# A hybrid decoder block: w_in multiplied with whole float32 numbers, the parameter chain early on VectorE, another order of the mixers' steps, narrow outputs

## Chip, cores and metric

One core of a Trainium2 chip runs one launch of the kernel. The metric is the device time of that launch in microseconds (us): for the kernel before, the median of three runs, 1183.16 us (1183.14 to 1184.67).

## What is computed

One trunk layer over 256 positions, model width 2048, in float32:

```
proj = rmsnorm(x, g1) @ w_in                     # 2048 x 3072: rg_u, rg_gate, s5_u, 1024 each
u  = causal_conv4(rg_u)                          # RG-LRU group, 16 heads of 64
r, i = sigmoid(u @ wa + ba), sigmoid(u @ wi + bi)
a  = exp(-8 r softplus(-lam));  h = scan(a, sqrt(1 - a^2) * i * u)
y_rg = gelu(rg_gate) * h
Abar = exp(A dt);  h = scan(Abar, ((Abar - 1) / A) B s5_u)   # S5 group, 64 groups of 64 complex states
y  = real(C h) + d * s5_u;  z = gelu(y);  y_s5 = z * sigmoid(z @ w_glu + b_glu)
x += concat(rmsnorm(y_rg), rmsnorm(y_s5)) @ w_out            # 2048 x 2048
h  = causal_conv3(rmsnorm(x, g2) @ w_up)                     # 2048 x 12288
x += (gelu(h[:6144]) * h[6144:]) @ w_down                    # 6144 x 2048
out = rmsnorm(x, gf)
```

## The kernel before

Channels lie on the 128 partitions, the 256 positions along the row. A weight matrix is cut into column tiles of 128 outputs; SyncE's queue loads it in blocks `raw` of 8 row tiles (128x1024 numbers, 512 KB) into four buffers. Exactness is kept by halves: ScalarE rounds a block to float32r (`wh`, L151), VectorE takes the remainder (`wl`, L154), and the activations are split the same way into a pair of high and low (`split`, L192 to L199). One row tile of a product, a *step*, is then either wide, one matmul of `wh` with both halves (128x512, L159) and one of `wl` with the high half (128x256, L163), or narrow, three matmuls of 128x256 (L161 to L163). The wide form leaves two halves in PSUM, which `total` adds (ScalarE copy L169, VectorE add L170). The letters in WIDE choose the form by matrix: A w_in, W and V the two halves of w_out, L w_glu, F w_up, D w_down. Steps: w_in 384, w_glu 64, w_out 256, w_up 1536, w_down 768.

The mixers' work is written as letters in ORDER, a letter with a tile's number: U a column of rg_u with its convolution, P its gates (`pg`), B decay and input of the recurrence for four tiles, G recurrence and gate column, S a column of s5_u, X the sines, T the tile's cosine and sine tables (six GpSimd operations), K its matrices (16 GpSimd operations `m`, `ball`, `cp`, transposes `tp`, products `cb`, and eight small loads `u4`), N the input `bu` and the scan, Y the output `y`, F and Z gelu and split, L the w_glu column, W and E, V the two halves of an output column; R and Q the two norms. The order is one of priority: a scheduler with its own idea of times places each instruction in its engine's in-order queue, so what `order` rows show below is fixed when the program is built. Before the tiles comes a chain of small operations on the parameters (L360 to L470), which gives the decay, the angles and the factors `fr`, `fi`, `nfr` that T and K read; its first exponential (`exp_parts`, called with G) runs on GpSimd. The first four columns of w_in (HEAD) take turns while x arrives in quarters `xq`; their PSUM tiles are all four buffers of `main`. x's squares are summed to `acc1`, and `rstd1` comes out of a product on TensorE (`ss`), a square root and a reciprocal.

Of the kernel before, what the change touches and what calls it, by code (L numbers as in the profile page):

```python
# [14 lines left out]
P = 128  # L15
# [14 lines left out]
# The mixers' steps in the order of their priority: a letter of block_kernel's steps and a tile's number.  # L30
ORDER = """
U0 P0 S0 U1 P1 U2 S1 X0 U3 T0 T1 P2 P3 U4 U5 S2 B0 U6 P4 U7 S3 P5 S4 K0 P6 P7 T2 B1 K1 N0 N1 Y0 S5 T3 Y1 F0 G0
K2 G1 G2 S6 T4 G3 G4 K3 F1 N2 T5 Y2 N3 G5 G6 Y3 F2 G7 S7 F3 K4 N4 R0 K5 N5 W0 Y4 T6 W1 W2 Y5 K6 Z0 Z1 E0 E1 W3
E2 E3 Z2 K7 Z3 F4 W4 E4 F5 W5 E5 N6 W6 E6 W7 E7 T7 W8 E8 N7 Y6 W9 Y7 W10 W11 E9 Z4 F6 E10 E11 Z5 W12 F7 E12 Z6
Z7 L0 W13 E13 L1 W14 E14 L2 L3 W15 L4 E15 L5 L6 L7 Q0 V0 V1 V2 V3 V4 V5 V6 V7 V8 V9 V10 V11 V12 V13 V14 V15
"""
# The columns of w_in that the first loads feed, and the order of those loads: a quarter of x or a block of w_in.
# [11 lines left out]
def _top(v, bits):  # L49
# [10 lines left out]
    ("g1", KX), ("g2", KX), ("gf", KX),  # L60
# [3 lines left out]
    ("logdt", NST), ("lam", KH), ("are", NST), ("aim", NST),  # L64
    ("step", NX + NY), ("ident", P),
]
COL = {}
# [8 lines left out]
def block_kernel(ctx, tc, a, out):  # L76
# [9 lines left out]
    # ---------------------------------------------------------------- constants  # L86
    par = cpool.tile([P, NCOL], F32, name="par")
    S.dma_start(par[:, :KX], a["par"][:, :KX])
# [13 lines left out]
    WIDE = "FDAWVL"  # L102
# [4 lines left out]
    CUT, CUT_END = 4, 3  # L107
# [8 lines left out]
    def fn(out, src, func, **kw):  # L116
        """An activation that needs its own table: these stay in program order, so that equal ones are neighbours."""
        ins = S.activation(out, src, func, **kw).ins  # L118
        if last_fn:
            tc.add_manual_dep(ins, last_fn[0].name, mybir.DependencyInfo(  # L120
                mybir.DependencyClass.NoSync, mybir.DependencyReason.DATA), reason="table order")
        last_fn[:] = [ins]

    # ------------------------------------------------------------- weight stream
    due = []

    def later(n, fn):
        """fn is emitted behind n more products."""
        due.append([n, fn])
# [18 lines left out]
    pieces = [1]  # L148

    def part(raw, wh, wl, k=slice(0, KC)):  # L150
        S.copy(wh[:, k, :], raw[:, k, :])  # L151
        n = (k.stop - k.start) // pieces[0]
        for i in range(k.start, k.stop, n):
            V.tensor_tensor(wl[:, i:i + n, :], raw[:, i:i + n, :], wh[:, i:i + n, :].bitcast(F32), ALU.subtract)  # L154

    def step(ps, wide, wh, wl, kk, x, first, last):
        """Adds w.T x of 128 rows; wide puts w_high x_low beside the rest."""
        if wide:
            PE.matmul(ps, lhsT=wh[:, kk, :], rhs=x, start=first, stop=False)  # L159
        else:  # L160
            PE.matmul(ps[:, 0, :], lhsT=wh[:, kk, :], rhs=x[:, 0, :], start=first, stop=False)  # L161
            PE.matmul(ps[:, 0, :], lhsT=wh[:, kk, :], rhs=x[:, 1, :], start=False, stop=False)  # L162
        PE.matmul(ps[:, 0, :], lhsT=wl[:, kk, :], rhs=x[:, 0, :], start=False, stop=last)  # L163
# [9 lines left out]
    def product(src, ot, kcs, xs, wide=False):  # L173
        """w.T x; a caller that wants it in PSUM takes the narrow one."""
# [3 lines left out]
        for kc in kcs:  # L178
            raw = load(src, ot, kc)
            wh, wl = w_parts()  # L180
            part(raw, wh, wl)
            for kk in range(KC):
                step(ps, wide, wh, wl, kk, xs[j], j == 0, j == n - 1)
                j += 1
        flush()
# [16 lines left out]
    def rstd(parts_, dim, tag):  # L202
        """1 / rms over the channels for every position, on all partitions; without a tag it stays in PSUM."""
# [17 lines left out]
    def rstd_direct(acc, dim, tag):  # L221
        """The same with one step on the tensor engine, more on the vector engine."""
# [17 lines left out]
    # ------------------------------------------------------------- split x  # L240
    # products that nobody reads raise the tensor engine's clock while the first loads run
# [5 lines left out]
    for name in HEAD_LOADS.split():  # L247
        if name == "p":
            nc.sync.dma_start(par[:, KX:], a["par"][:, KX:])
            continue  # L250
# [5 lines left out]
        else:  # L256
            if o == 0:
                raw0[i] = wpool.tile([P, KC, P], F32, tag="raw", name="raw", bufs=4)
            nc.sync.dma_start(raw0[i][:, o:o + n, :], a["w_in"][HEAD[i % len(HEAD)], i // len(HEAD), :, o:o + n, :])

    def x_split(k):
        xs.append(split(cpool, f"x{k}", xq[k // 4][:, k % 4, :], col("g1", k), V if k in XV else S))

    # ===================================================================== mixers
    with ExitStack() as ph:
# [3 lines left out]
        # the first columns' products take turns by the rows of x, as these arrive  # L269
        early = {c: psm.tile([P, 2, T], F32, tag="main", name="ps") for c in HEAD}  # L270
        acc1 = mix.tile([P, 4, T], F32, tag="e4", name="acc1")
        for i in range(2 * len(HEAD)):
            kc, ci = divmod(i, len(HEAD))
            ps = early[HEAD[ci]]
            wh, wl = w_parts()
            n = KC // 2 if ci == 0 else KC
            for r in range(0, KC, n):
                ks = range(KC * kc + r, KC * kc + r + n)
                if ci == 0:
                    x_split(ks[0])  # L280
                part(raw0[i], wh, wl, slice(r, r + n))
                if ci == 0:
                    for k in ks[1:]:
                        x_split(k)
# [5 lines left out]
                for k in ks:  # L290
                    step(ps, "A" in WIDE, wh, wl, k % KC, xs[k], k == 0, k == KX - 1)
# [4 lines left out]
        # short steps let the chain of small ones on the parameters through  # L296
        pieces[0] = CUT

        # -------------------------------------------------- small parameter math
        ahead = tc.high_priority(offset=PRI)  # L300
        ahead.__enter__()
        # what the scans' tiles hold before them
# [12 lines left out]
        def stt(e, out, x, c, y, op0, op1):  # L315
            """(x op0 c) op1 y"""
# [46 lines left out]
        p0, s0, s1 = exp_parts(G, e_in, nE, "d")  # L363
        ex = tl(nE, "ex")
        stt(G, ex, p0, 1.0, s0, ALU.add, ALU.mult)
        G.tensor_tensor(ex, ex, s1, ALU.mult)
# [6 lines left out]
        # angle of one step, into [-pi, pi]  # L373
# [9 lines left out]
        # angle of a block of steps, in turns, as a short part and its rest; the four state tiles of a channel tile as s5_scan has them  # L383
# [9 lines left out]
        # cosine and sine at the multiples of NY blocks and at those below it  # L393
# [29 lines left out]
        # decay of a block, in s5_scan's order of the state tiles  # L423
# [7 lines left out]
        # powers 3, 2, 1 of A  # L431
# [13 lines left out]
        def times(ore, oim, xre_, xim_, yre, yim, t):  # L445
            """A product of complex numbers; t has the place of two."""
# [9 lines left out]
        # factors of b by the position in the block: A^(3 - position) (A - 1) / a; the real part negated as well  # L456
# [29 lines left out]
        def s5_tables(c):  # L486
            """Cosine and sine at every block."""
# [12 lines left out]
        def s5_mats(c):  # L500
# [7 lines left out]
            # b for the four positions, [imaginary, tile, channel, position]  # L508
# [9 lines left out]
            # c A^3, c A^2, c A  # L518
# [27 lines left out]
            # a head's channels by position in the rows, two heads at a time  # L546
# [54 lines left out]
        # softplus(-lambda) times -4  # L601
# [16 lines left out]
        # ------------------------------------------------------------- the mixers' steps  # L618
# [10 lines left out]
        def w_in_col(o):  # L629
            wide = "A" in WIDE  # L630
            return total(early[o] if o in early else product(a["w_in"], o, (0, 1), xs, wide), wide)

        def rg_u(j):
            """Column tile j of u, and its convolution."""
            if j == CUT_END:
                pieces[0] = 1
# [12 lines left out]
        def rg_gates(j):  # L649
            """Its two gates; r in tau, i times u in bu."""  # L650
# [12 lines left out]
        def rg_batch(g):  # L663
            """Decay and input of the recurrence, for four tiles."""
# [6 lines left out]
            # 1 / (1 - tanh) is (1 + a) / 2: one Newton step from the exponential's (1 + a) / 2; it and h come out negated  # L671
# [9 lines left out]
        def rg_out(j):  # L681
            """The recurrence, the gate's column tile and their product."""
# [25 lines left out]
        def rg_top(o):  # L708
            """The RG-LRU half of the output's column tile o."""
# [24 lines left out]
        def s5_top(o):  # L734
            """The S5 half, and the second norm's input."""
# [22 lines left out]
    # ======================================================================== FFN  # L758
# [48 lines left out]
# ---- layout of the arrays for the launch  # L807
# [87 lines left out]
```

## Time and profile before

| | |
|---|---|
| median of the timed runs | 1183.16 us |
| profiled execution, span from first to last instruction | 1181.2 us |
| TensorE busy | 1119.9 us (95%) |
| VectorE, ScalarE, GpSimd busy | 892.4, 641.0, 270.8 us |
| mean granted TensorE clock | 0.98 |
| chain that ended last | TensorE 80%, GpSimd 9%, VectorE 7% |

The page gives busy time by engine, and the chain of work that ended last, followed back from the last instruction. TensorE's matmuls overlap in the records, so their busy times add up to more than the span; how long a step takes is read from the distance of starts. Everything outside the first third (slices 1 to 11 of 40) shows TensorE at nine tenths and more.

### The profile page before, as it was taken

What the parts mean: (1) busy time and instruction counts of PE and PEld (TensorE: products, weight loads), DVE (VectorE), ACT (ScalarE), POOL (GpSimd) and SP (SyncE); (2) the same over time, 40 slices, a digit from 0 to 9 for tenths busy, and PEclk for the clock granted to TensorE, in tenths of its full rate; (3) what the DMA queues carried; (4) which work ended last, traced back from release to release, by engine and by line L of the source; (5) the groups of instructions that cost most, each with busy time, mean ns of one, the idle gap of its engine ahead of it and who ended that gap; (6) DMA issues with size and microseconds to landing.
All of it is one profiled execution on the core that took longest, in us unless ns stands there. A gap on an engine that the chain in (4) does not pass through costs nothing.

```text
span 1181.2 us, 18986 instructions
## 1 busy us (share of the span) xinstructions
PE 1119.9 (95%) x7134; PEld 973.9 (82%) x7134; DVE 892.4 (76%) x1356; ACT 641.0 (54%) x1014; POOL 270.8 (23%) x300
## 2 busy tenths in 40 slices
PE   7887869879999999999999999999999999999996
PEld 6775658767888888888888888888888888888886
DVE  6899999997899887787787777877876444445443
ACT  6475655534876655555555555555554444344432
POOL 6368997893333000000000000000000000000000
PEclk8999889999999999999999999999999999999998
DMA  7554336443656666666666666666666666666662
GB/s 255 163 168 136 109 118 195 143 131 99 196 178 191 187 193 189 189 193 186 191 193 187 190 194 186 192 192 187 192 191 185 189 184 187 187 186 190 183 191 90
DMA packets 65980, 209.25 MB, mean 177 GB/s; under 512 B 12000, under 2 KB 15584, under 8 KB 65888
## 3 DMA queue, kind: packets, MB, share of 16 engines
q1 hardware_dynamic: 65744, 208.03, 58.5%
q8 instruction: 56, 0.92, 0.3%
q14 instruction: 36, 0.29, 0.1%
q10 hardware_dynamic: 144, 0.01, 0.0%
HBM read 204.87 MB, written 2.10 MB: 175 GB/s over the span
## 4 chain that ended last, share of the span: by engine, by line
PE 80%; POOL 9%; DVE 7%; issue 2%; ACT 1%; DMA 1%; SPq 0%; DVEq 0%; POOLq 0%; ACTq 0%
PE ps L159 51%; PE ps L163 27%; DVE wl L154 2%; POOL cp L528 1%; DVE wa L574 1%; POOL m L516 1%; POOL ball L517 1%; DVE xq L685 1%; ACT wh L151 1%; DMA xq<-in_xT 1%; POOL m L515 1%; POOL m L525 0%; PE ps L162 0%; DVE rcv L643 0%; PE ps L161 0%
## 5 line engine op out<-in xcount | busy, mean ns | idle before, releaser
L159 PE MATMUL ps<-sp,wh 128*128 128x512 f32 x2960 | 1043.9, 396 | 3.8 <-ACT wh L151 1.9
L163 PE MATMUL ps<-sp,wl 128*128 128x256 f32 x3008 | 851.3, 283 | 18.2 <-DVE wl L154 18.2
L159 PEld LDWEIGHTS ps<-sp,wh 128*128 128x128 f32 x2960 | 558.4, 189 | 130.0 <-DVE sp L199 2.5
L154 DVE TENSOR_TENSOR wl<-raw,wh 128x1024 fp32r<-128x1024 f32 (+2 forms) x384 | 478.5, 1248 | 234.4 <-ACT wh L151 232.7
L151 ACT CAST wh<-raw 128x1024 fp32r<-128x1024 f32 (+1 forms) x378 | 395.0, 1046 | 411.2 <-PE ps L159 286.2
L163 PEld LDWEIGHTS ps<-sp,wl 128*128 128x128 f32 x3008 | 572.3, 190 | 25.9 <-DVE wl L154 23.7
L236 POOL TENSOR_TENSOR accx<-accx,sq 128x256 f32<-128x256 f32 x29 | 37.7, 1301 | 793.6 <-ACT sq L235 793.5
L770 DVE SCALAR_TENSOR_TENSOR cv<-u,par,cv 128x255 f32<-128x255 f32 x192 | 92.1, 481 | 3.7 <-ACT cv L768 0.3
L170 DVE TENSOR_TENSOR t<-t,ps 128x256 f32<-128x256 f32 x160 | 65.7, 412 | 0.1
L169 ACT COPY t<-ps 128x256 f32<-128x256 f32 x160 | 57.8, 363 | 10.0 <-DVE u L720 7.6
L768 ACT ACTIVATE cv<-u,par 128x256 f32<-128x256 f32 x96 | 57.1, 596 | 1.4 <-DVE u L766 1.4
L766 DVE TENSOR_TENSOR u<-t,rstd 128x256 f32<-128x256 f32 x96 | 40.4, 421 | 1.6
L528 POOL TENSOR_TENSOR cp<-m,m 64x192 f32<-64x192 f32 x32 | 31.1, 973 | 1.9
L788 DVE TENSOR_TENSOR xq<-xq,ps 128x256 f32<-128x256 f32 x31 | 13.0, 421 | 16.4 <-PE ps L163 15.9
L721 POOL TENSOR_TENSOR xq<-xq,u 128x256 f32<-128x256 f32 x16 | 18.0, 1127 | 26.4 <-DVE u L720 20.8
L118 ACT ACT_TABLE_LOAD x17 | 21.8, 1283 | 1.4 <-PEq L884 1.2
L780 DVE TENSOR_TENSOR hv<-ge,cv 128x256 f32<-128x256 f32 x48 | 20.4, 426 | 1.9 <-issue 0.2
L118 ACT ACTIVATE ge<-cv 128x256 f32<-128x256 f32 x48 | 20.1, 419 | 0.2
L193 DVE TENSOR_TENSOR sp<-hv,sp 128x256 fp32r<-128x256 f32 x48 | 20.1, 419 | 0.0
L531 ACT COPY bp<-ball 64x128 f32<-64x128 f32 x16 | 6.8, 423 | 24.3 <-POOL ball L517 24.2
L192 ACT CAST sp<-hv 128x256 fp32r<-128x256 f32 x48 | 19.5, 406 | 0.0
L199 DVE SCALAR_TENSOR_TENSOR sp<-xq,par,sp 128x256 fp32r<-128x256 f32 x32 | 15.6, 521 | 1.5 <-ACT sp L198 1.5
(245 smaller groups left out, 654.2 us busy)
## 6 DMA issues: line engine op xcount, KB each, us to landing
raw<-in_w_up SPq DMA_DIRECT2D x192, 512.0 KB, 4.3
raw<-in_w_down SPq DMA_DIRECT2D x96, 512.0 KB, 4.3
raw<-in_w_in SPq DMA_DIRECT2D x47, 512.0 KB, 4.2
raw<-in_w_out SPq DMA_DIRECT2D x32, 512.0 KB, 4.1
raw<-in_w_glu SPq DMA_DIRECT2D x8, 512.0 KB, 4.1
xq<-in_xT SPq DMA_DIRECT2D x7, 512.0 KB, 6.0
out_y<-xq SPq DMA_DIRECT2D x6, 256.0 KB, 2.1
rw<-in_rgw SPq DMA_DIRECT2D x8, 128.0 KB, 3.5
```

The source lines that it names most:

```text
L118: ins = S.activation(out, src, func, **kw).ins
L151: S.copy(wh[:, k, :], raw[:, k, :])
L154: V.tensor_tensor(wl[:, i:i + n, :], raw[:, i:i + n, :], wh[:, i:i + n, :].bitcast(F32), ALU.subtract)
L159: PE.matmul(ps, lhsT=wh[:, kk, :], rhs=x, start=first, stop=False)
L163: PE.matmul(ps[:, 0, :], lhsT=wl[:, kk, :], rhs=x[:, 0, :], start=False, stop=last)
L169: S.copy(t, ps[:, 1, :])
L170: V.tensor_tensor(t, t, ps[:, 0, :], ALU.add)
L236: G.tensor_tensor(acc, acc, q, ALU.add)
L528: G.tensor_tensor(cp[rp, :BL - 1, m, :, 16 * h:16 * h + 16], m1[rp], m2[rp], op)
L766: V.tensor_tensor(u, ps, rs["n2"], ALU.mult)
L768: S.activation(cv, u, AF.Identity, bias=col("fcb", o), scale=col("fcw", 2 * 2 * KF + o))
L770: V.scalar_tensor_tensor(cv[:, d:], u[:, :T - d], col("fcw", (2 - d) * 2 * KF + o), cv[:, d:], ALU.mult, ALU.add)
```

## The change

All 384 steps of w_in take the loaded block as it is: one float32 matmul of 128x256, without `wh`, `wl` and without splitting x (`x_scale` only multiplies by g1). w_glu and w_out become narrow (WIDE is "FD"), so their results are read from PSUM without `total`. The columns that the parameter chain reads move to the front of `par`, in the first load on ScalarE's queue (136 columns instead of 16; the second load, on SyncE's queue, has 632 instead of 752). The first exponential runs on VectorE. The cutting of `wl` into pieces (CUT) goes. ORDER is another.

```diff
-U0 P0 S0 U1 P1 U2 S1 X0 U3 T0 T1 P2 P3 U4 U5 S2 B0 U6 P4 U7 S3 P5 S4 K0 P6 P7 T2 B1 K1 N0 N1 Y0 S5 T3 Y1 F0 G0
+U0 X0 S0 P0 U1 P1 T0 K0 U2 P2 S1 N0 Y0 U3 P3 B0 T1 K1 U4 P4 S2 N1 Y1 U5 P5 T2 K2 U6 P6 S3 N2 Y2 U7 P7 B1 T3 K3 F0
...
-    ("g1", KX), ("g2", KX), ("gf", KX),
+    ("g1", KX), ("logdt", NST), ("lam", KH), ("are", NST), ("aim", NST), ("step", NX + NY),
+    ("g2", KX), ("gf", KX),
...
-    S.dma_start(par[:, :KX], a["par"][:, :KX])
+    S.dma_start(par[:, :NFIRST], a["par"][:, :NFIRST])
...
-    WIDE = "FDAWVL"
+    WIDE = "FD"
...
+    def product_whole(src, ot, kcs, x):
+        ps = psm.tile([P, T], F32, tag="main", name="ps")
+        n = len(kcs) * KC
+        for i, kc in enumerate(kcs):
+            raw = load(src, ot, kc)
+            for kk in range(KC):
+                j = KC * i + kk
+                PE.matmul(ps, lhsT=raw[:, kk, :], rhs=x[j], start=j == 0, stop=j == n - 1)
+        flush()
+        return ps
...
+    def x_scale(k):
...
+        if k in XV:
+            V.tensor_scalar(xs[k], src, col("g1", k), None, ALU.mult)
+        else:
+            S.activation(xs[k], src, AF.Copy, scale=col("g1", k))
...
-                    step(ps, "A" in WIDE, wh, wl, k % KC, xs[k], k == 0, k == KX - 1)
+                    PE.matmul(ps, lhsT=raw0[i][:, k % KC, :], rhs=xs[k], start=k == 0, stop=k == KX - 1)
...
-        p0, s0, s1 = exp_parts(G, e_in, nE, "d")
+        p0, s0, s1 = exp_parts(V, e_in, nE, "d")
...
-            wide = "A" in WIDE
-            return total(early[o] if o in early else product(a["w_in"], o, (0, 1), xs, wide), wide)
+            return early[o] if o in early else product_whole(a["w_in"], o, (0, 1), xs)
```

TensorE's queue, before, where tile 0's `cb` and `bu` stand (`u` the tile's input, rows with `sp` and `wh` or `wl` are halves of steps):

```order
L159 MATMUL ps<-sp,wh 128x512
L163 MATMUL ps<-sp,wl 128x256
L541 MATMUL cb<-cp_511,bp_510 32x96 x8
L562 MATMUL bu<-u_1217,bt 64x64 x16
L163 MATMUL ps<-sp,wl 128x256
```

They stand some 400 rows into that queue, and tile 0's transposes `tp`, ahead of them, come after 193 steps. In the changed queue `tp` begins after 85 float32 steps (rows `ps<-xg,raw`), of which 64 are the first four columns, and the rows behind these 64 are:

```order
L193 MATMUL ps<-xg,raw 128x256 x9
L664 MATMUL pg<-rcv,rw 128x256 x2
L193 MATMUL ps<-xg,raw 128x256 x12
L664 MATMUL pg<-rcv,rw 128x256 x2
L545 MATMUL tp<-par,ball 128x128 x2
L193 MATMUL ps<-xg,raw 128x256 x6
L545 MATMUL tp<-par,ball 128x128 x2
L193 MATMUL ps<-xg,raw 128x256 x4
L664 MATMUL pg<-rcv,rw 128x256 x2
L193 MATMUL ps<-xg,raw 128x256 x5
L551 MATMUL cb<-cp_383,bp_382 32x96 x8
L572 MATMUL bu<-u_520,bt 64x64 x16
```

From tile 2 on a tile's `tp`, `cb` and `y` stand among about 48 steps. GpSimd's queue, before, between the end of the parameter chain and the first table (`room` holds the parameters, `xq<-ig` is P's last step):

```order
L321 TENSOR_SCALAR room<-room 128x32
L322 TENSOR_TENSOR room<-room 128x32
L392 TENSOR_SCALAR room<-room 128x32
L661 TENSOR_TENSOR xq_547<-ig,rcv 128x256 x2
L496 TENSOR_TENSOR tm<-xs 128x256
```

The same place in the changed queue, and the beginning of tile 0's matrices, 14 rows after the first table row:

```order
L332 TENSOR_TENSOR room<-room 128x32
L402 TENSOR_SCALAR room<-room 128x32
L506 TENSOR_TENSOR tm<-xs 128x256
L505 TENSOR_TENSOR cs_t<-xc 128x256
```

```order
L525 TENSOR_TENSOR m_476<-pk,fr 128x256
L526 TENSOR_TENSOR m_477<-pk,fi 128x256
L506 TENSOR_TENSOR tm<-xs 128x256
L527 TENSOR_TENSOR ball<-m_476,m_477 128x4x4x16
L507 TENSOR_TENSOR cs_t<-cs_t,tm 128x256
```

Nothing of P stands between the chain and the tables any more, and the chain's first exponential, 30 rows of GpSimd's queue before, is gone from it.

## Rows read from the trace of the kernel before

**Rows 1.** Windows: us, then busy us of each engine, granted clock, DMA share.

```profile
0.00:70.00 70.00, 59.55 (x307) 50.29 (x308) 54.18 (x144) 41.50 (x63) 34.34 (x71) 0.95 0.65 214
...
90.00:165.00 75.00, 53.27 (x471) 42.84 (x470) 70.54 (x78) 42.16 (x79) 70.59 (x65) 0.89 0.38 115
...
200.00:270.00 70.00, 56.60 (x590) 46.61 (x590) 63.57 (x84) 34.31 (x72) 64.04 (x72) 0.93 0.45 136
...
sum 345.00, PE 293.80 PEld 246.22 DVE 308.30 ACT 201.50 POOL 237.21; mean PE 48.97 PEld 41.04 DVE 51.38 ACT 33.58 POOL 39.53
```

**Rows 2.** Waits of TensorE, 0 to 345 us: total, times, longest.

```profile
PE ps L163 <- DVE wl L154: 18.2, 17, 3.1
PE cb L541 <- POOL cp L528: 8.8, 3, 6.6
PE tp L535 <- POOL ball L517: 5.0, 3, 3.0
...
PE y L589 <- DVE wx L578: 2.5, 3, 2.2
```

**Rows 3.** Chain that ended last, two gate products (float32): start, us.

```profile
60.14 0.86 PE pg L657 x4
```

**Rows 4.** The same chain, last wide step and first narrow one.

```profile
1151.95 0.23 PE ps L159
1152.18 0.12 PE ps L163
1152.30 0.12 PE ps L161
1152.41 0.12 PE ps L162
```

**Rows 5.** Weight loads of the gate products, by source line: ns min/median/max.

```profile
L657 PEld LDWEIGHTS pg<-rcv,rw x32: 186/189/338, 59.9 to 132.3; 128*128 128x128 f32 x32
```

**Rows 6.** Groups of instructions, 0 to 330 us: busy, mean ns, idle before.

```profile
L154 DVE TENSOR_TENSOR wl<-raw,wh 128x1024 fp32r<-128x1024 f32 x73 | 106.7, 1464 | 11.1 <-ACT wh L151 10.9
...
L685 DVE TENSOR_TENSOR_SCAN xq<-xq,xq 128x256 f32<-128x256 f32 x8 | 8.4, 1110 | 2.3 <-POOL xq L679 2.3
```

**Rows 7.** GpSimd's busy time from 90 to 270 us.

```profile
90.00:270.00 180.00, 163.54 (x162) 0.93 0.45 136
```

**Rows 8.** One line of K by source line: ns min/median/max, first and last start.

```profile
L515 POOL TENSOR_TENSOR m<-pk,fr x8: 645/751/1627, 91.7 to 257.7; 128x256 f32<-128x256 f32 x8
```

**Rows 9.** Timeline of the start and of the parameter chain: start, us, engine.

```profile
4.05 0.35 DVE L196 TENSOR_SCALAR sp<-xq,par 128x256 fp32r<-128x256 f32 x1 [4.05 <-DMA par<-in_par]
...
9.53 1.71 ACT L198 ACTIVATE sp<-xq,par 128x256 fp32r<-128x256 f32 x4 [1.14 <-DMA xq<-in_xT]
...
11.78 0.18 DVE L360 COPY room<-par 128x32 f32<-128x32 f32 x1
11.88 0.17 DVE L361 TENSOR_SCALAR room<-par 128x8 f32<-128x8 f32 x1
...
36.53 0.30 POOL L321 TENSOR_SCALAR room<-room 128x32 f32<-128x32 f32 x1
36.91 0.25 POOL L322 TENSOR_TENSOR room<-room 128x32 f32<-128x32 f32 x1
...
68.33 1.28 ACT L118 ACT_TABLE_LOAD   x1
69.62 0.63 ACT L118 ACTIVATE xs<-xs 128x512 f32<-128x512 f32 x1
70.33 0.70 POOL L496 TENSOR_TENSOR tm<-xs 128x256 f32<-128x256 f32 x1
```

**Rows 10.** Timeline of TensorE, one tile's `tp`, `cb` and `bu`.

```profile
267.76 1.09 PE L535 MATMUL tp<-par,ball 128*128 128x128 f32 x4 [3.78 <-ACT cb L545]
273.80 0.54 PE L541 MATMUL cb<-cp,bp 128*32 128x96 f32 x16
274.26 0.69 PE L562 MATMUL bu<-u,bt 64*64 64x64 f32 x32
```

More of the change, by code (lines that the diff above doesn't have):

```diff
@@ L31 @@
 ORDER = """
-U0 P0 S0 U1 P1 U2 S1 X0 U3 T0 T1 P2 P3 U4 U5 S2 B0 U6 P4 U7 S3 P5 S4 K0 P6 P7 T2 B1 K1 N0 N1 Y0 S5 T3 Y1 F0 G0
-K2 G1 G2 S6 T4 G3 G4 K3 F1 N2 T5 Y2 N3 G5 G6 Y3 F2 G7 S7 F3 K4 N4 R0 K5 N5 W0 Y4 T6 W1 W2 Y5 K6 Z0 Z1 E0 E1 W3
-E2 E3 Z2 K7 Z3 F4 W4 E4 F5 W5 E5 N6 W6 E6 W7 E7 T7 W8 E8 N7 Y6 W9 Y7 W10 W11 E9 Z4 F6 E10 E11 Z5 W12 F7 E12 Z6
-Z7 L0 W13 E13 L1 W14 E14 L2 L3 W15 L4 E15 L5 L6 L7 Q0 V0 V1 V2 V3 V4 V5 V6 V7 V8 V9 V10 V11 V12 V13 V14 V15
+U0 X0 S0 P0 U1 P1 T0 K0 U2 P2 S1 N0 Y0 U3 P3 B0 T1 K1 U4 P4 S2 N1 Y1 U5 P5 T2 K2 U6 P6 S3 N2 Y2 U7 P7 B1 T3 K3 F0
+F1 F2 G0 S4 N3 Y3 F3 T4 K4 G1 G2 S5 N4 Y4 F4 T5 K5 G3 G4 S6 N5 Y5 F5 T6 K6 G5 G6 S7 N6 Y6 F6 T7 K7 G7 N7 Y7 F7 R0
+W0 Z0 Z1 E0 W1 Z2 Z3 E1 W2 Z4 Z5 E2 W3 Z6 Z7 E3 L0 L1 W4 E4 L2 L3 W5 E5 L4 L5 W6 E6 L6 L7 W7 E7 W8 E8 W9 E9 Q0 W10
+E10 W11 E11 W12 E12 W13 E13 W14 E14 W15 E15 V0 V1 V2 V3 V4 V5 V6 V7 V8 V9 V10 V11 V12 V13 V14 V15
 """
@@ L63 @@
     ("fcw", 3 * 2 * KF), ("fcb", 2 * KF),
-    ("logdt", NST), ("lam", KH), ("are", NST), ("aim", NST),
-    ("step", NX + NY), ("ident", P),
+    ("ident", P),
 ]
+NFIRST = KX + 3 * NST + KH + NX + NY
 COL = {}
@@ L106, in block_kernel @@
     WARM = 12
-    CUT, CUT_END = 4, 3
+    RAW = 4
     PRI = 400
@@ L138, in load @@
     def load(src, ot, kc):
-        raw = wpool.tile([P, KC, P], F32, tag="raw", name="raw", bufs=4)
+        raw = wpool.tile([P, KC, P], F32, tag="raw", name="raw", bufs=RAW)
         nc.sync.dma_start(raw, src[ot, kc])
@@ L146, in w_parts, with part @@
         return wh, wl
[L148 to L154, printed above, removed]
+    def part(raw, wh, wl):
+        S.copy(wh, raw)
+        V.tensor_tensor(wl, raw, wh.bitcast(F32), ALU.subtract)
     def step(ps, wide, wh, wl, kk, x, first, last):
@@ L248, in block_kernel @@
         if name == "p":
-            nc.sync.dma_start(par[:, KX:], a["par"][:, KX:])
+            nc.sync.dma_start(par[:, NFIRST:], a["par"][:, NFIRST:])
             continue
@@ L257, in block_kernel @@
             if o == 0:
-                raw0[i] = wpool.tile([P, KC, P], F32, tag="raw", name="raw", bufs=4)
+                raw0[i] = wpool.tile([P, KC, P], F32, tag="raw", name="raw", bufs=RAW)
             nc.sync.dma_start(raw0[i][:, o:o + n, :], a["w_in"][HEAD[i % len(HEAD)], i // len(HEAD), :, o:o + n, :])
-    def x_split(k):
-        xs.append(split(cpool, f"x{k}", xq[k // 4][:, k % 4, :], col("g1", k), V if k in XV else S))
+    def x_scale(k):
+        if k % 2 == 0:
+            pair = cpool.tile([P, 2, T], F32, tag=f"x{KH + k // 2}", name="xg")
+            xs.extend((pair[:, 0, :], pair[:, 1, :]))
+        src = xq[k // 4][:, k % 4, :]
+        if k in XV:
+            V.tensor_scalar(xs[k], src, col("g1", k), None, ALU.mult)
+        else:
+            S.activation(xs[k], src, AF.Copy, scale=col("g1", k))
     with ExitStack() as ph:
@@ L267, in block_kernel @@
         mw = ph.enter_context(tc.tile_pool(name="mw", bufs=2))
-        early = {c: psm.tile([P, 2, T], F32, tag="main", name="ps") for c in HEAD}
+        early = {c: psm.tile([P, T], F32, tag="main", name="ps") for c in HEAD}
         acc1 = mix.tile([P, 4, T], F32, tag="e4", name="acc1")
@@ L274, in block_kernel @@
             ps = early[HEAD[ci]]
-            wh, wl = w_parts()
             n = KC // 2 if ci == 0 else KC
@@ L279, in block_kernel @@
                 if ci == 0:
[L280 to L284, printed above, removed]
+                    for k in ks:
+                        x_scale(k)
                     t = ks[0] // 4
@@ L295, in block_kernel @@
             rstd1 = rstd_direct(acc1[:, 0, :], D, "rstd1")
-        pieces[0] = CUT
         ahead = tc.high_priority(offset=PRI)
@@ L362, in block_kernel @@
         V.tensor_tensor(e_in[:, NST:nE], e_in[:, NST:nE], lamc, ALU.min)
-        p0, s0, s1 = exp_parts(G, e_in, nE, "d")
+        p0, s0, s1 = exp_parts(V, e_in, nE, "d")
         ex = tl(nE, "ex")
-        stt(G, ex, p0, 1.0, s0, ALU.add, ALU.mult)
-        G.tensor_tensor(ex, ex, s1, ALU.mult)
+        stt(V, ex, p0, 1.0, s0, ALU.add, ALU.mult)
+        V.tensor_tensor(ex, ex, s1, ALU.mult)
         dt = ex[:, 0:NST]
@@ L629, in w_in_col @@
         def w_in_col(o):
-            wide = "A" in WIDE
-            return total(early[o] if o in early else product(a["w_in"], o, (0, 1), xs, wide), wide)
+            return early[o] if o in early else product_whole(a["w_in"], o, (0, 1), xs)
         def rg_u(j):
-            if j == CUT_END:
-                pieces[0] = 1
             ps = w_in_col(j)
```

## Prediction

> **What bounds the kernel now.** I read the windows first. Up to 345 us TensorE is busy for 293.8 of 345 us, and the granted clock is below 1 in the stretches where it is idle most (0.89 from 90 to 165 us, 0.93 from 200 to 270) [rows 1]; behind that nothing but matmuls stands in the chain that ended last. So a microsecond saved or lost before 345 us moves the end by one, and the feed-forward part, which the change leaves alone, needs no sum. Then the list of waits: TensorE waits most for the remainders `wl` of VectorE (18.2 us) and for GpSimd's matrices (`cp` 8.8, `ball` 5.0) [rows 2]. VectorE is busy 70.5 of the 75 us from 90 to 165, GpSimd 70.6 [rows 1]: both are full at once, while TensorE has 21.7 us idle. The front part is thus held by the two helpers, and the change takes work from them and gives it to TensorE.
>
> **What w_in costs.** Two gate products, each one float32 matmul of 128x256, take 0.86 us for their four passes, 0.43 us per matmul [rows 3]. A wide step takes 0.23 + 0.12 = 0.35 [rows 4]. All 384 steps of w_in change from one to the other: 384 x 0.43 = 165.1 against 384 x 0.35 = 134.4, 30.7 us more on the engine that sets the end. It is a stream of such matmuls, which this trace has only in groups of two; between the passes lie weight loads of 189 ns [rows 5], shorter than a pass of 215, and I take them as hidden as they are in that group.
>
> **Narrow outputs.** The first narrow step behind the wide ones goes on at 0.12, 0.12 per piece, so three pieces cost about 0.35, as a wide step does [rows 4]: 320 steps at no difference on TensorE. One copy and one addition per result go from ScalarE and VectorE; they were not what TensorE waited for there, so I count nothing.
>
> **What VectorE and GpSimd get rid of.** The 48 blocks of w_in no longer need `wh` and `wl`; a `wl` is 1.46 us in the front part [rows 6], 70 us of VectorE's 308 [rows 1]. The wait of 18.2 us for `wl` goes where it belongs to w_in. What is late next is GpSimd, so its chain has to be followed.
>
> **The parameter chain.** Before, it starts when the second load of `par` lands, 11.78 us, and the first table operation runs at 70.33 [rows 9]. Now its columns come in the first load, which before lets the scaling of x begin at 4.05 us [rows 9]; 68 KB instead of 8 may add half a microsecond, which the fourth step's wait for x below hides. VectorE's small operations follow each other at 0.10 us, GpSimd's pairs at 0.37 per operation [rows 9]. So: 4.1 + about 40 on VectorE (4) + 24 on GpSimd (9) + two sums of squares between them (2 x 2.4, on GpSimd as before) + eight wide VectorE operations (5) = 27 us. The sines stand on ScalarE behind the square root of `rstd1`, and that waits for TensorE's `ss`, which follows 47 steps. x's second quarter lands at 9.53 us [rows 9], one scaling later four steps are done and 43 follow: 9.96 + 43 x 0.43 = 28.5. With `ss` 0.4, root 0.5, table load 1.3, two short sines 0.6, a wide one 0.6 and the other 0.7 the tables begin at about 33 us. The chain is 37 us earlier than before.
>
> **The ramp behind it.** The first four columns end at 9.96 + 60 x 0.43 = 35.8. TensorE comes to the first `tp` after 21 more steps and two gate products, at 46.5. GpSimd needs 18 operations to the first half of `ball`. At 0.8 us each, between the shortest 0.65 and the median 0.75 and mean near 1 of such lines [rows 8], that is 33 + 14.4 = 47.4 or a little more with the start of its queue: wait 1.3. The second half (6 operations, 52.6) against six steps and two transposes (tp 1.09 for four, cb 0.54, bu 0.69 [rows 10]): wait 1.7. `cb` (11 operations, 61.4) against nine steps and a gate product: wait 3.5. The second tile likewise 0.4 and 1.1. Sum 8 us. After that a tile has about 48 steps, 20.6 us, and some 7 us of its small matmuls, 28 us together, whereas GpSimd does 163.5 us in 180 for eight tiles [rows 7], 20.4 a tile: TensorE sets the pace, and GpSimd gets ahead.
>
> The Trainium skill, "SBUF — State Buffer", section "Who interferes with whom", says that a VectorE instruction with two inputs in SBUF keeps GpSimd from reading. The spread of one line of K, 645 to 1627 ns, agrees [rows 8]. By that rule GpSimd's operations would shrink to about 0.65 us once `wl`, two inputs, is gone, and the 8 us of the ramp would vanish; the forecast keeps 0.8.
>
> **The sum.** Lost before, up to 345 us: 51.2 us idle, and the work at the lower clock, 59.6 x 0.05 + 53.3 x 0.11 + 56.6 x 0.07 = 12.8 [rows 1], together 64.0. Lost after, estimated: start 3.1 (1.6 before the first step, 1.5 for x's second quarter), ramp 8, one place where the four scans of the recurrence (1.11 us each [rows 6]) stand between a tile's `bu` and `y` on VectorE 3, the start of w_out, whose four PSUM tiles wait for the norm, 2, single waits like those for `wx` [rows 2] 4: 20.1 idle. Clock loss in the proportion of before, 12.8 / 51.2 = 0.25 per idle microsecond: 5.0. Together 25.1. The change is 30.7 + 25.1 - 64.0 = -8.2 us: the profiled span of 1181.2 becomes 1173.0. The timed median stands 2.0 above that span, so the time is 1175.0 us. It breaks even where the loss after is 33 us.
>
> **The SyncE queue.** `u4`'s eight loads stand behind loads of `raw` that wait for a free buffer, now released by the last matmul instead of by `wl`. Four buffers are 4 x 8 x 0.43 = 13.8 us of work, so I count nothing; if that cover is gone, each tile's `bu` is late by up to a block, 3.4 us.
>
> **Rivals.**
> 1. A float32 step takes more in a long stream. fp32r pieces run at 0.12 us per 256 columns, slower than the pass of 0.215 per 512 [rows 3, 4]; if the passes came at that rate a step is 0.47. Price 384 x 0.04 = 15.4, time 1190. It decides from 0.43 + 8.2/384 = 0.451 us per step on: slower than before. For it: only groups of two are seen. Against it: in these the four passes fit 0.215 each. Chance 0.13.
> 2. Weight loads that are not hidden. Four loads of 0.189 beside 0.86 would give 0.81 per step, (0.86 + 4 x 0.189) / 2, 384 x 0.38 = 145 us, time 1320. The gate products show them hidden [rows 3, 5]. Chance 0.02. The Trainium skill, "TensorE: Matmul & The Clock Gate", section "Weight-path perf modes", says that the fast weight load is off for float32; the trace does not bear out a price for it, since the loads of both types take about 190 ns.
> 3. GpSimd or an in-order queue still holds TensorE. If the 36.6 us that TensorE is idle from 90 to 270 us stayed by half, 18 x 1.25 = 23 us come on top: 1198. For it: the order comes from a scheduler's own times. Against it: 20.4 against 28 us a tile. Chance 0.09.
> 4. The helpers' loss shrinks by no more than w_in costs, loss after 31 to 35 us: 1183. Chance 0.10.
> 5. The waits vanish but for the start: loss 10, 30.7 + 10 - 64.0 = -23, 1160. Short GpSimd operations speak for it. Chance 0.16.
>
> The forecast has 0.50. A measurement of this kernel can tell 0.2%, 2.4 us, from no change. Faster is the forecast and rival 5, 0.66; the same rival 4, 0.10; slower rivals 1 to 3, 0.24. The forecast's own range is 1165 to 1181 (ramp 0 to 12 us); the range for 8 in 10 goes from rival 5 to a little beyond rival 1, 1159 to 1192.
>
> **What would show it.** Steps of w_in start 0.43 us apart; no `wl` before w_out; the first table operation near 33 us and the first `ball` near 47; TensorE idle about 20 us in the front part, mostly at `tp` and `cb` before 75 us; granted clock 1 from then on. The forecast is wrong if steps come 0.45 us apart or more, if tables begin behind 45 us, or if `cb`, `y` or `bu` still wait after the third tile.

## The result: 1172.9 us, and the profile after

The changed kernel takes 1172.9 us (median of four, 1169.79 to 1174.26) against 1183.74 for the kernel before, run beside it: a ratio of 0.9902 [0.9886, 0.9917], 10.8 us less. The forecast was 1175.0. The profiled span went from 1181.2 to 1172.4 us, 8.8 less; the forecast said 8.2 less. The profiled execution is the slowest of the four and has the lowest granted clock, 0.988; the fastest, 1169.79 us, has 0.994.

First the windows of after, in the columns of [rows 1] and over the same stretches, then two finer stretches and the sum to 345 us:

```profile
0.00:70.00 70.00, 65.47 (x392) 56.07 (x396) 50.94 (x161) 26.53 (x52) 52.55 (x91) 1.00 0.57 190
90.00:165.00 75.00, 64.88 (x554) 54.52 (x547) 47.21 (x64) 27.51 (x63) 53.76 (x65) 0.89 0.42 134
200.00:270.00 70.00, 67.72 (x684) 61.52 (x683) 42.90 (x68) 29.93 (x56) 14.32 (x19) 0.98 0.52 159
...
75.00:110.00 35.00, 31.76 (x262) 26.37 (x262) 26.17 (x31) 16.16 (x34) 31.91 (x37) 0.90 0.43 136
150.00:190.00 40.00, 34.87 (x311) 29.43 (x312) 21.59 (x33) 9.24 (x25) 28.33 (x39) 0.87 0.48 148
...
sum 345.00, PE 327.97 PEld 293.44 DVE 234.51 ACT 143.95 POOL 186.17; mean PE 46.85 PEld 41.92 DVE 33.50 ACT 20.56 POOL 26.60
```

TensorE is busy for 328.0 of the first 345 us, before 293.8; VectorE went from 308.3 to 234.5, GpSimd from 237.2 to 186.2. The two finer stretches, 75 to 110 and 150 to 190 us, are where TensorE is still idle most and the granted clock lowest. The waits of TensorE there (0 to 360 us: total, times, longest):

```profile
PE y L599 <- DVE wx L588: 6.7, 1, 6.7
PE y L599 <- ACT ig L119: 3.2, 1, 3.2
PE tp L545 <- POOL ball L527: 2.2, 3, 0.8
PE ps L158 <- DVE u L727: 1.9, 1, 1.9
PE cb L551 <- POOL cp L538: 1.1, 1, 1.1
```

The 18.2 us for `wl` at the head of [rows 2] are gone, and the waits for GpSimd's `cp` and `ball` fell from 13.8 to 3.3. At the head stands one wait of 6.7 us that was not in that list at this size.

The chain that ended last has the new steps of w_in as a stream (start, us, how many passes; one step shows as two passes in the trace). From three places of it:

```profile
8.78 18.83 PE ps L304 x86
...
104.00 3.86 PE ps L193 x12
...
187.85 7.34 PE ps L193 x34
```

43 steps in 18.83 us are 0.438 each, 17 in 7.34 are 0.432. The six behind the wait at 104 take 0.64 each; that stretch has the granted clock of 0.90.

The early chain, in ScalarE's and GpSimd's timeline (start, us, idle before and what ended it):

```profile
28.08 0.47 ACT L119 ACTIVATE rstd<-ss,eps_t 128x256 f32<-128x256 f32 x1 [0.52 <-PE ss L233]
...
30.12 0.61 ACT L119 ACTIVATE xs<-xs 128x512 f32<-128x512 f32 x1
30.82 0.63 POOL L506 TENSOR_TENSOR tm<-xs 128x256 f32<-128x256 f32 x1 [6.04 <-ACT xs L119]
43.73 1.12 POOL L525 TENSOR_TENSOR m<-pk,fr 128x256 f32<-128x256 f32 x1 [2.47 <-DVE fr L461]
46.18 0.73 POOL L527 TENSOR_TENSOR ball<-m,m 128x256 f32<-128x256 f32 x1
```

The first table operation is at 30.8 us instead of 70.3 [rows 9], and the first `ball` ends at 46.9.

### The profile page after: what moved, and what is told of

Its sections match the earlier page's. It is cut to its first block, busy times and chain, and to the rows that moved or that the text cites. A ratio compares the mean times of both kernels' runs of the same rounds, so it can differ in the third digit from the quotient of the medians.

```text
span 1172.4 us, 19286 instructions
## 1 busy us (share of the span) xinstructions
PE 1145.3 (98%) x7454; PEld 1014.7 (87%) x7454; DVE 805.4 (69%) x1246; ACT 574.3 (49%) x897; POOL 209.7 (18%) x270
## 4 chain that ended last, share of the span: by engine, by line
PE 88%; DVE 4%; POOL 4%; DMA 1%; issue 1%; ACT 1%; SPq 0%; DVEq 0%; ACTq 0%; POOLq 0%
PE ps L156 44%; PE ps L160 27%; PE ps L193 6%; PE ps L159 4%; PE ps L158 4%; PE ps L304 2%; PE y L602 1%; PE y L607 1%; POOL m L525 1%; DMA xq<-in_xT 0%; POOL cp L538 0%; DVE wa L584 0%; POOL m L526 0%; DVE xq L806 0%; POOL tm L506 0%
## 5 line engine op out<-in xcount | busy, mean ns | idle before, releaser
L156 PE MATMUL ps<-sp,wh 128*128 128x512 f32 x2256 | 787.1, 393 | 0.0
L160 PE MATMUL ps<-sp,wl 128*128 128x256 f32 x2624 | 738.0, 281 | 0.0
L151 DVE TENSOR_TENSOR wl<-raw,wh 128x1024 fp32r<-128x1024 f32 x328 | 403.8, 1231 | 245.1 <-ACT wh L150 243.7
L150 ACT CAST wh<-raw 128x1024 fp32r<-128x1024 f32 x328 | 344.8, 1051 | 429.2 <-PE ps L156 251.8
L160 PEld LDWEIGHTS ps<-sp,wl 128*128 128x128 f32 x2624 | 496.6, 189 | 0.0
L193 PE MATMUL ps<-xg,raw 128*128 128x256 f32 x640 | 146.5, 385 | 0.0
L193 PEld LDWEIGHTS ps<-xg,raw 128*128 128x128 f32 x640 | 121.1, 192 | 17.5 <-issue 0.3
L158 PE MATMUL ps<-sp,wh 128*128 128x256 f32 x368 | 104.6, 285 | 1.9 <-DVE u L727 1.9
L159 PE MATMUL ps<-sp,wh 128*128 128x256 f32 x368 | 104.8, 285 | 0.1
L773 DVE TENSOR_TENSOR u<-t,rstd 128x256 f32<-128x256 f32 x96 | 40.4, 421 | 1.6
L167 DVE TENSOR_TENSOR t<-t,ps 128x256 f32<-128x256 f32 x96 | 39.7, 414 | 0.0
L166 ACT COPY t<-ps 128x256 f32<-128x256 f32 x96 | 34.7, 361 | 0.0
L304 PE MATMUL ps<-xg,raw 128*128 128x256 f32 x128 | 28.7, 384 | 0.2 <-ACT xg L279 0.2
L304 PEld LDWEIGHTS ps<-xg,raw 128*128 128x128 f32 x128 | 24.5, 193 | 4.0 <-ACT xg L279 0.6
```

The costliest lines, as they stand in the source:

```text
L150: S.copy(wh, raw)
L151: V.tensor_tensor(wl, raw, wh.bitcast(F32), ALU.subtract)
L167: V.tensor_tensor(t, t, ps[:, 0, :], ALU.add)
L193: PE.matmul(ps, lhsT=raw[:, kk, :], rhs=x[j], start=j == 0, stop=j == n - 1)
L304: PE.matmul(ps, lhsT=raw0[i][:, k % KC, :], rhs=xs[k], start=k == 0, stop=k == KX - 1)
L773: V.tensor_tensor(u, ps, rs["n2"], ALU.mult)
```

## Experiments

The theory is that whole numbers take VectorE and GpSimd off the path, and that nearly all of the gain comes from this. Rivals: the gain is the early chain's, the new order's or the narrow outputs'. The first group takes one part out of the changed kernel, the second puts one part alone into the kernel before, the third tries to remove the waits that are left. Ratios, with their 95% intervals, are to the kernel before on the same chip. Some of the profiles are compared at one landmark: the start of a given result of w_up on VectorE (`u<-t,rstd`, L773 in after), of which there are 96.

**Whole numbers out of the changed kernel.** The kernel before with the three other parts:

```diff
...
+NFIRST = KX + 3 * NST + KH + NX + NY
...
-    WIDE = "FDAWVL"
+    WIDE = "FDA"
...
-        p0, s0, s1 = exp_parts(G, e_in, nE, "d")
+        p0, s0, s1 = exp_parts(V, e_in, nE, "d")
...
```

> The changed kernel with w_in again in halves (wide steps, wh and wl, x split); the early parameter chain, the new order and the narrow outputs stay. My theory: w_in as whole numbers pays by taking 48 remainders of about 1.2 to 1.5 us and 24 sums from VectorE. With them back VectorE is full in the front part again and TensorE waits for wl: 34 us less matmul work (384 x 0.09), but waits as before or more, time 1172 to 1190. Rival, order and chain alone make the gain and whole numbers only cost their matmul time: 1140 to 1150.

1199.56 us, 1.0133 [1.0118, 1.0148]. VectorE's busy time up to 345 us, then TensorE's waits:

```profile
0.00:345.00 345.00, 293.75 (x473) 0.94 0.46 148
```

```profile
PE ps L164 <- DVE wl L155: 18.9, 13, 2.9
PE cb L542 <- POOL cp L529: 9.5, 5, 3.0
PE tp L536 <- POOL ball L518: 8.8, 6, 2.5
```

This is above the range expected. Without whole numbers the rest of the change costs 16 us; with them it ends 27 us lower. The list is that of [rows 2] again.

**The old order in the changed kernel.**

```diff
-U0 X0 S0 P0 U1 P1 T0 K0 ...
+U0 P0 S0 U1 P1 U2 S1 X0 ...
```

> The changed kernel with the step order of before, all else as changed. My theory: the old order brings tile 0's matrices late and lets S5 run on beside w_out, but TensorE is now the slow engine, so 5 to 15 us are lost: 1178 to 1188. Rival, the order does not matter once w_in is whole: 1171 to 1175. Rival, the order is the main part of the gain: above 1195.

1173.12 us, 0.9910 [0.9896, 0.9925]: no difference from the changed kernel. Beside whole numbers the order is worth nothing that can be measured; the first rival held, not the theory.

**The late chain in the changed kernel.**

```diff
-    S.dma_start(par[:, :NFIRST], a["par"][:, :NFIRST])
+    S.dma_start(par[:, :KX], a["par"][:, :KX])
...
-        p0, s0, s1 = exp_parts(V, e_in, nE, "d")
+        p0, s0, s1 = exp_parts(G, e_in, nE, "d")
```

> The changed kernel with the parameter columns in the second load and the first exponential on GpSimd, as before. My theory: the chain starts 8 us later and takes 30 operations of 0.37 us more on GpSimd, so the tables begin at 48 to 52 instead of 31 us and tile 0's transposes are awaited: 10 to 18 us slower than changed, 1183 to 1191. Rival, the tables were held by the square root behind ss, not by the chain, and the loss is under 4 us: 1173 to 1177.

1176.47 us, 0.9943 [0.9928, 0.9958], so the early chain gives 3.6 us here by the medians and 4.9 by the ratios; the rival's range held. The tables by source line (ns min/median/max, first and last start):

```profile
L505 POOL TENSOR_TENSOR tm<-xs x8: 617/626/1488, 45.3 to 154.1; 128x256 f32<-128x256 f32 x8
```

They begin 14.5 us later, and the time moves by a quarter to a third of that.

**Wide outputs in the changed kernel.**

```diff
-    WIDE = "FD"
+    WIDE = "FDWVL"
```

> The changed kernel with w_glu and w_out wide again (with the copy and the sum of the halves). In the changed trace a narrow step takes 0.36 us, a wide one 0.35. My theory: no cost hidden there either way, 320 steps x 0.00 to 0.01: 1169 to 1173. Rival, the copies and sums were waited for at the start of w_out and w_glu: 1175 to 1180.

1176.55 us, 0.9945 [0.9928, 0.9961]: 3.6 us slower than the changed kernel by the medians, 5.1 by the ratios, where the prediction counted nothing. Starts in the chains speak the other way: eight wide steps there take 2.77 us, 0.346 each, and a narrow step of after is three passes of 0.12, so 320 narrow steps should cost 4.5 us. From the chain of after:

```profile
299.88 0.12 PE ps L160
300.00 0.12 PE ps L158
300.12 0.12 PE ps L159
```

The traces show what repays it. First the results of w_up from the twelfth on, then the wide halves of w_up's steps from 600 to 800 us, each time wide outputs above and after below (ns min/median/max, first and last start):

```profile
L773 DVE TENSOR_TENSOR u<-t,rstd x85: 412/424/428, 418.0 to 893.1; 128x256 f32<-128x256 f32 x85
L773 DVE TENSOR_TENSOR u<-t,rstd x85: 415/424/427, 426.0 to 891.9; 128x256 f32<-128x256 f32 x85
```

```profile
L156 PE MATMUL ps<-sp,wh x568: 395/398/403, 599.6 to 800.0; 128*128 128x512 f32 x190
L156 PE MATMUL ps<-sp,wh x578: 391/391/391, 599.7 to 799.7; 128*128 128x512 f32 x193
```

At the twelfth result the kernel with wide outputs is 8.0 us ahead. Some 4 us of this, an estimate from the windows, are a higher granted clock in that execution (0.95, 0.91 and 1.00 from 75 to 110, 150 to 190 and 230 to 260 us, for 0.90, 0.87 and 0.94); the rest fits the 4.5 us of the narrow steps. Then it loses 9.2 us in w_up, 475.1 us for 465.9, whose code is the same in both: 0.353 us per step for 0.347, with no wait and a granted clock of 1. Why these steps are slower is not shown. So the narrow outputs do not pay by the copies and sums that they save, and the rival had the range but not the cause.

**Whole numbers alone, in the kernel before.**

```diff
...
-                    step(ps, "A" in WIDE, wh, wl, k % KC, xs[k], k == 0, k == KX - 1)
+                    PE.matmul(ps, lhsT=raw0[i][:, k % KC, :], rhs=xs[k], start=k == 0, stop=k == KX - 1)
...
```

> The kernel before with whole w_in alone: old order, old parameter chain, wide outputs. Undoing the order cost the changed kernel nothing, undoing the chain 3.6 us, undoing the narrow outputs 3.7. My theory: whole numbers are nearly the entire gain, and the parts add up: 1172.9 + 7 = 1178 to 1182. Rival, whole numbers need the early chain to pay, since GpSimd then still paces the front part: 1184 or more.

1174.09 us, 0.9934 [0.9913, 0.9955], before 1181.61 on that chip. This is below the range expected: the parts do not add up. TensorE's longest waits up to 360 us:

```profile
PE y L598 <- DVE wx L587: 7.5, 2, 4.9
PE cb L550 <- POOL cp L537: 6.4, 3, 2.8
```

One part by itself brings two thirds of the gain, 7.5 of 10.8 us (its interval just reaches the changed kernel's). In the profiled executions the twelfth result of w_up starts at 434.6 us before, 426.8 here and 426.0 in after, so that up to there it brings 7.8 of 8.6 us. VectorE is busy for 227.0 of the first 345 us, and of the waits for `wl` one of 0.8 us is left, in w_out.

**The new order alone.** Only ORDER is replaced in the kernel before.

> The kernel before with the new order alone. With w_in in halves and all the rest new the time was 1199.6. My theory: the new order asks for tile 0's matrices and for two things per tile from a VectorE that is full, so it is what loses there: 1195 to 1210. Rival, that loss came from the early chain on VectorE or from the narrow outputs: 1180 to 1187.

1206.84 us, 1.0212 [1.0191, 1.0233].

```profile
PE ps L163 <- DVE wl L154: 17.2, 15, 2.5
PE cb L541 <- POOL cp L528: 12.0, 6, 3.7
PE cb L541 <- issue: 9.4, 1, 9.4
PE tp L535 <- POOL ball L517: 6.9, 5, 2.2
```

With VectorE full the new order puts `cb` and `tp` ahead of what GpSimd can deliver. But this accounts for only a part of the 25 us. The results of w_up from the twelfth on:

```profile
L766 DVE TENSOR_TENSOR u<-t,rstd x85: 414/424/427, 448.6 to 923.4; 128x256 f32<-128x256 f32 x85
```

In the kernel before they start from 434.6 to 900.5 us. So the profiled execution is 14.0 us behind at the twelfth result, and it loses another 8.9 in w_up, at the slower pace seen with wide outputs above. Of the fourteen kernels only these two, with the new order and a wide w_out, show that pace. The same letters cost nothing once w_in is whole and w_out narrow.

**The early chain alone.** The edit of the late chain the other way round, in the kernel before.

> The kernel before with the early parameter chain alone (columns in the first load, first exponential on VectorE). In the changed kernel undoing the chain cost 3.6 us. My theory: before, the tables were held by VectorE's queue, where the chain's eight wide operations lie between remainders of 1.2 us (39.6 to 61.8 us), so an earlier start is partly eaten: 2 to 8 us faster, 1174 to 1180. Rival, VectorE is full and the chain on it delays wl: 1182 to 1190.

1183.21 us, 0.9993 [0.9984, 1.0002]: nothing, and not the 2 to 8 us expected. The tables begin 3.4 us earlier, not 37. They stand in GpSimd's queue behind P's last steps, and these wait for the gates' sigmoids (timeline of this kernel):

```profile
59.88 0.77 POOL L662 TENSOR_TENSOR xq<-ig,rcv 128x256 f32<-128x256 f32 x1 [23.73 <-ACT ig L119]
64.92 1.88 POOL L662 TENSOR_TENSOR xq<-ig,rcv 128x256 f32<-128x256 f32 x1 [4.27 <-ACT ig L119]
66.87 0.70 POOL L497 TENSOR_TENSOR tm<-xs 128x256 f32<-128x256 f32 x1
```

GpSimd is idle for 28.0 us ahead of the two rows of P, and the sines that the tables read stand on ScalarE behind the same sigmoids (66.15 us). So in the old order the time at which `par` lands does not decide when the tables begin.

**Attack on the wait for `wx`.** It ends last because of VectorE's queue (timeline of after):

```profile
141.12 4.14 DVE L202 TENSOR_TENSOR sp<-us,sp 128x256 fp32r<-128x256 f32 x3
...
149.95 4.22 DVE L692 TENSOR_TENSOR_SCAN xq<-xq,xq 128x256 f32<-128x256 f32 x4
154.09 0.66 DVE L588 TENSOR_TENSOR wx<-wx,wb 128x256 f32<-128x256 f32 x1
```

Four scans of the recurrence stand just ahead of the addition that TensorE waits for. The edit gives the tile's scan a higher priority and moves two GpSimd products of the recurrence to VectorE:

```diff
...
+            with tc.high_priority(offset=PRI):
+                return s5_scan_(*args)
...
-            G.tensor_tensor(b4, b4, q4, ALU.mult)
-            G.tensor_tensor(b4, b4, tau, ALU.mult)
+            V.tensor_tensor(b4, b4, q4, ALU.mult)
+            V.tensor_tensor(b4, b4, tau, ALU.mult)
```

> The changed kernel with two places of waiting taken away: the two products of the recurrence's input (128x1024, L685 and L686) on VectorE instead of GpSimd, and each tile's scan at a higher priority, so that the four scans of the recurrence no longer stand inside it. My theory: the waits of 6.7 and 3.2 us for y go, and with them most of the time at half clock behind them: 1162 to 1168. Rival, they are replaced by others on VectorE, which the products load with 5 us more: 1171 to 1175.

1179.35 us (ten runs), 0.9974 [0.9961, 0.9986]: slower than the changed kernel, above both ranges. The wait for `wx` is gone, and the other wait for `y` has grown. TensorE at the second tile's `y`, in after and here:

```profile
100.24 0.65 PE L599 MATMUL y<-wx,cp 128*32 128x64 f32 x16 [3.24 <-ACT ig L119]
...
100.30 0.65 PE L603 MATMUL y<-wx,cp 128*32 128x64 f32 x16 [9.44 <-ACT ig L119]
```

It starts at the same time in both. In after 30 passes of w_in (6.74 us) stand between `cb` and this `y` and fill most of the time; here `y` follows `bu` with no step between. `y` and the gate products `pg` share one PSUM buffer (tag "y"), so a `y` has to wait until the sigmoids have read `pg`. What holds the sigmoids is GpSimd, in after by the second of the two products, here by `ball`, whose copy stands ahead of them in ScalarE's queue with a table load of 1.28 us behind it (ScalarE in after, then here):

```profile
99.35 0.47 ACT L119 ACTIVATE tau<-pg,par 128x256 f32<-128x256 f32 x1 [5.59 <-POOL xq L686]
...
97.25 0.86 ACT L541 COPY bp<-ball 64x128 f32<-64x128 f32 x2 [4.72 <-POOL ball L527]
```

The edit changes two things at once; their shares in the 6.5 us (by the medians) were not separated.

**`pg` out of that buffer.**

```diff
-            pg = ps1.tile([P, 2, T], F32, tag="y", name="pg")
+            pg = psm.tile([P, 2, T], F32, tag="main", name="pg")
```

> The changed kernel with the gate products in the PSUM buffers of w_in instead of the one they share with y. My theory: the wait of 3.2 us for y behind the gates' sigmoid goes, the built order also takes the four scans of the recurrence out of a tile's scan, so the 6.7 us go too, and part of the clock loss: 1160 to 1168. Rival, other waits take their place, as when the two products went to VectorE: 1171 to 1178.

1192.13 us, 1.0068 [1.0051, 1.0085], slower than before the change and above both ranges:

```profile
PE pg L664 <- DVE rcv L650: 6.9, 4, 3.6
PE cb L551 <- POOL cp L538: 6.8, 3, 2.7
```

Three pairs of gate products now stand right behind the first four columns on TensorE and wait for their convolutions. The shared buffer, at which 3.2 us were waited, seems to have kept them back; no run separates this from the use of w_in's own PSUM buffers by `pg`.

**A sixth of w_in by halves again.** In the eight gate columns the first eight steps are narrow, the other eight whole (64 of 384 steps), since VectorE now has room:

```diff
...
+            for k in range(KC):
+                h, l = xsplit[k][:, 0, :], xsplit[k][:, 1, :]
+                PE.matmul(ps, lhsT=wh[:, k, :], rhs=h, start=k == 0, stop=False)
+                PE.matmul(ps, lhsT=wh[:, k, :], rhs=l, start=False, stop=False)
+                PE.matmul(ps, lhsT=wl[:, k, :], rhs=h, start=False, stop=False)
...
-            ps = w_in_col(8 + j)
+            ps = product_mixed(8 + j)
```

> The changed kernel with the first half of each gate column of w_in (8 columns x 8 steps) in halves again, narrow, beside whole second halves. My theory: VectorE has room there (about 60% busy from 150 to 230 us), 64 steps at 0.36 instead of 0.44 us save 5 us of TensorE: 1166 to 1170. Rival, the eight remainders and eight splits of x bring back waits for wl: 1173 to 1180.

1168.70 us (1168.42 to 1169.07), 0.9889 [0.9869, 0.9909]. It is the fastest kernel of the study by its median, but its interval overlaps the changed kernel's, 0.9902 [0.9886, 0.9917], so that the two are not told apart as ratios. 64 steps shorter by 0.08 us are 5 us, and the twelfth result of w_up starts 5.8 us earlier (420.2 for 426.0); VectorE has 249.4 us in 345 instead of 234.5, and TensorE's longest wait is 6.1 us, for `wx` as in after.

**The combinations.** Mixed columns with `pg` moved, and then the scan's priority as well:

> The gate products moved as in d_pg, and the first half of each gate column of w_in in halves. My theory: the two gains add, 4 us of steps and 5 to 12 us of waits: 1157 to 1164. Rival, more work on VectorE brings waits back: 1166 to 1172.

> d_mixpg with each tile's scan at a higher priority. My theory: no more than d_mixpg, since there the scans are apart already: within 3 us of it. Rival, wx comes late in d_mixpg at other tiles and priority takes another 3 to 6 us.

1189.83 us, 1.0051 [1.0036, 1.0066], and 1207.19 us, 1.0199 [1.0184, 1.0214]. Both keep the loss of moving `pg`, so neither theory held. In the second, whose list follows, there are also waits for the loads of the tile's input, 6.7 us for 0.3 in the first:

```profile
PE pg L669 <- DVE rcv L655: 8.1, 4, 5.9
PE bu L576 <- DMA u<-us: 6.7, 3, 5.3
```

## Why the prediction was right

The cause it named was the cause: w_in's halves had VectorE and GpSimd full, and whole numbers trade that for more matmul time. Whole numbers alone bring two thirds of the gain, and the waits for `wl` go with them. Taking them out of the changed kernel turns the gain into a loss, but that loss is in part the new order's, which loses by itself beside full helpers. That the sum came within 2.1 us of the time is partly luck, as its steps show:

- **The price of a step, right.** 0.43 forecast, 0.432 to 0.438 measured over 17 and 43 steps: against a wide step of 0.346 (0.35 forecast) that is 384 x 0.086 to 0.092 = 33.0 to 35.3 us for 30.7. Rival 1 wanted 0.451. (It speaks of passes of 512 columns; the rows give a pass as 128x256.) Weight loads stay hidden (rival 2): each of 190 ns lies beside a pass of about 216. That the halves' loads take as long says little on rival 2's rule, since both kinds hold 32-bit numbers.
- **The loss after, right in sum: 25.5 for 25.1, by errors that cancel.** Idle 345 - 328.0 = 17.0 us (forecast 20.1): the start 1.2 for 3.1, the ramp 3.3 for 8, the scans 6.7 for 3, the start of w_out 1.9 for 2, single waits 3.7 for 4. Lower clock 64.9 x 0.11 + 67.7 x 0.02 = 8.5 (forecast 5.0). I had said that the clock would be 1 from the ramp on; it is 0.90 and 0.87 in the stretches around the two long waits.
- **The chain, right to the tables, luck behind them.** First table operation 30.8 for 33, held by the square root behind `ss`, as argued. First `ball` at 46.9 for 47.4, but not by GpSimd alone: the sum ended the chain at 27 us, and `fr`, which the matrices read, left VectorE only at 43.7. GpSimd waited 2.5 us for it (the row at 43.73 above). The sum had no such wait.
- **The ramp, too long: 3.3 us for 8.** I gave GpSimd 0.8 us per operation. Up to the first `ball` that was near, 0.76 over 18 operations without the wait for `fr`; behind it 17 operations take 10.5 us, 0.62 each, and `cp` is done at 57.4 instead of 61.4. The two stretches in the columns of [rows 1], and the line of K that had a median of 751 ns [rows 8]:

```profile
30.80:46.90 16.10, 15.40 (x72) 13.10 (x70) 14.85 (x45) 4.26 (x7) 13.14 (x19) 1.00 0.48 160
46.90:57.40 10.50, 8.52 (x46) 6.80 (x46) 2.28 (x4) 3.60 (x8) 10.18 (x18) 1.00 0.34 89
```

```profile
L525 POOL TENSOR_TENSOR m<-pk,fr x8: 639/646/1122, 43.7 to 185.5; 128x256 f32<-128x256 f32 x8
```

  GpSimd is faster where VectorE runs little, 2.3 of 10.5 us. The section "Who interferes with whom" of the Trainium skill's "SBUF — State Buffer" says that a VectorE instruction with two inputs in SBUF contends with a GpSimd instruction that reads SBUF; the trace agrees with that rule rather than with one price of 0.8 throughout.
- **The recurrence's scans, too short: 6.7 us for 3.** The four scans in one place were foreseen, but not that VectorE comes to them late, behind three splits of 4.14 us. The other 3.2 us, at `y` behind the sigmoids, were within my 4 for single waits, but I had not seen the shared buffer.
- **`y` still waits after the third tile**, which I had named as a sign that the forecast is wrong. It happens once, and 6.7 us is too little to turn the sign; as a criterion it lacked a price.
- **Early chain and order, not separated.** I priced the change as one sum. Alone they are worth 0 and -25 us (9 of these in w_up), beside whole numbers 3.6 and 0.
- **Narrow outputs: 0 forecast.** By their starts they cost 4.5 us. That the changed kernel is 3.6 us slower without them comes from w_up, which no sum had.
- **The loss before, too small at 64.0.** I counted idle time and the clock alone; what that leaves out follows.

With the measured terms the sum does not close: 33.0 to 35.3 for w_in, 4.5 for the narrow outputs and 25.5 - 64.0 give -1.0 to +1.3 us, and the span fell by 8.8. The gain is complete early in the feed-forward part: the twelfth result of w_up (VectorE, L766 before and L773 after) starts at 434.6 and 426.0, the last at 900.5 and 891.9, both 8.6 us apart. TensorE shows no idle time and the clock of 1 between 345 us and there, in both kernels. So some 8 to 10 us are missing in the first 345. The starts of all matmuls there show most of it. With idle time and the stretches at the lower clock left out, a wide step of before is on the mean 0.365 us long from start to next start (616 steps), not 0.346: 11 to 12 us that count as busy. The records hide them: that of a wide step's first matmul is 0.39 us long and the next start 0.23 behind, so a wait of up to 0.16 us shows no idle time. Such short waits, 44 of about 0.1 us, are 4.6 us, and the hidden beginnings of 22 longer ones 4.2. After, the float32 steps have 0.442 over 378 steps, 1.5 to 3.8 us above the 0.432 to 0.438 counted, and the narrow ones 0.363, 0.9 us. So before lost some 6 to 9 us more than after in waiting that counts as busy, most of what is missing. What stays open is what each of these short waits was for.

## What to carry to other kernels

Before a part of a change is priced by itself, see whether the engine that it relieves or loads is full: the same order of work cost 14 us in the front part beside full helpers and nothing beside free ones. A longer instruction on the engine that sets the end pays when it takes a full helper off its path; price it by the distance of starts, over a whole stretch and not from one undisturbed place, and bound what remains by the helper's own busy time per tile. Before a difference is given a cause, see at a landmark in which part of the program it arises: two kernels here lost 9 us in a part that no edit touched. A wait at the head of the list is not a gift of its size: the edit that removed the one of 6.7 us let the next grow from 3.2 to 9.4, and undoing the shared buffer behind that cost 19.

## What the runs showed of the hardware

VectorE and GpSimd take longer beside each other, on both sides. GpSimd's side is in the ramp above. For VectorE's: three splits that take 0.42 us each at 235.5 us took 4.14 together at 141.1 us of after, the first 2.58 beside a long product on GpSimd, the other two 1.64 beside shorter ones:

```profile
140.61 2.81 POOL L686 TENSOR_TENSOR xq<-xq,tau 128x1024 f32<-128x1024 f32 x1
141.12 2.58 DVE L202 TENSOR_TENSOR sp<-us,sp 128x256 fp32r<-128x256 f32 x1
...
235.54 0.42 DVE L202 TENSOR_TENSOR sp<-us,sp 128x256 fp32r<-128x256 f32 x1
```

The section of the Trainium skill named above, "Who interferes with whom" in "SBUF — State Buffer", says that the order of issue decides which of the two blocks. Here the product started half a microsecond ahead of the first split, which ended 0.3 us behind it; that agrees.

The same wide step of w_up took 0.347 us in twelve of the fourteen kernels and 0.353 in two, all at a granted clock of 1 and with no wait. Its cause is not shown; from the twelfth result to the last it made 9 us.
